# One decoder layer in split fp32: operands moved to one byte offset modulo 256, transposes grouped four to a PSUM bank, and a few tasks listed in another order

## The chip, the cores and the metric

The kernel runs on one core of a Trainium2 chip. The metric is device time in microseconds (us), the median of three runs. Lower is better.

## The reference

One layer of a hybrid decoder on 512 tokens with 1024 features:

```
h = swiglu(rms_norm(x), w_gate, w_up, w_down)      # ffn1, 2816 wide
x = x + 0.5 * rms_norm(h)
u = rms_norm(x)
... = split(u @ w_in)                               # inputs of three token mixers
merged = g0 * (o_nsa @ w_nsa) + g1 * (o_dn @ w_dn) + g2 * (o_mem @ w_mem),  g = sigmoid(u @ w_branch_gate)
x = x + rms_norm(merged @ w_out)
h = swiglu(rms_norm(x), ...)                        # ffn2
x = x + 0.5 * rms_norm(h)
```

The three mixers are an 8-head sparse attention over compressed, selected and window keys, a gated DeltaNet with 4 heads of 128, and a 4-head cross-attention into 256 memory tokens. Everything is fp32 outside; all weights are read once.

## The kernel before

**Split products.** Every large product is done as three matmuls in the type fp32r. Each operand is split into a rounded part (hi, made by ScalarE) and a rest (lo, made by VectorE or GpSimd), and `mm3` (L114 to L119) issues hi x hi (L117), hi x lo (L118) and lo x hi (L119). A weight tile of 128x512 comes through `wload` (L89 to L110): a DMA into `wraw`, a ScalarE copy into `whi` (L106), a subtraction into `wlo` (L109).

Two patterns use `mm3`. In `prod_fm` the weights are the stationary operand (128 columns of `whi` or `wlo`) and the tokens move (`xth`, `xtl`, `odh`, `omth`, `onh`: 256 or 512 columns). In `down_half` the hidden parts `Hh`, `Hl` are stationary and the weights move (512 columns). So each matmul reads two SBUF operands: its moving one, and, while it streams, the stationary one of the matmul after it is being loaded.

**The fast phase.** From the fifth feature tile on, each FFN forms its gate and up products from seven smaller products instead of eight (`fast_tile`, L419 to L450): per feature tile 7 products x 4 slices x 3 = 84 matmuls of 256 columns, all at L429. Their stationary operands lie in two sets of tiles used in turn (`fset`, and `fxth` with `fxtl`), cut out by `fast_set` at an offset of OFFW elements; the moving ones are `thi` and the low parts in `txa`, `txb`, `tmth`, `tmtl`. 16 tiles in each of the two FFNs go this way.

**Where the operands lie.** SBUF pools are laid out one behind the other in each partition, so a tile's byte offset is the sum of the sizes ahead of it. The pool `cp` holds `xth` and `xtl`, then `RB`, then `mth` (2144 fp32 elements = 8576 bytes = 33.5 x 256), then `mtl`; the pools with weights, hidden tiles and the mixers come behind `mtl`. In the built program the offsets modulo 256 are:

| operand | before |
|---|---|
| `xth`, `xtl`, `mth` (also `odh`, `omth`, `tmth`), `ringh` | 0 |
| `mtl` (also `odl`, `omtl`, `tmtl`), `thi`, `txa`, `txb`, `onh`, `onl` | 128 |
| `whi`, `wlo`, `Hh`, `Hl` | 128 |
| set `fset` | 64 |
| set `fxth`, `fxtl` | 192 |

(`ringh` is the buffer for the moving weights of ffn2's down products, laid over `xtl`.) All strides in these operands are multiples of 512 bytes, so the offset modulo 256 is that of every slice.

**Transposes.** `transp` (L190 to L204) turns normalised tokens into features. For each feature tile k it takes a PSUM bank, transposes two token tiles into half of it (L198), and empties it with ScalarE into hi (L200), VectorE into lo (L201) and in some places ScalarE once more into a full fp32 copy (L203). It is called in seven places: the start of ffn1 (`feat`, twice four times), the memory tokens, the mixers' input (twice), and the input of ffn2 (twice).

**Order.** Work is issued as tasks in lists (`order_s` at the start, `order0` around ffn1's end, `order` and `order2` in the mixers, `order3` behind them). `off` lifts some of them by a priority offset, and a scheduler lays out each engine's instructions from that. All loads go through SyncE's queue (SP).

Of the kernel before, what the change touches and what calls it, by code (L numbers as in the profile page):

```python
# [10 lines left out]
F32 = mybir.dt.float32  # L11
# [19 lines left out]

C_ID, C_TRI, C_NEG, C_LVL, C_EYE, C_END = 0, 128, 256, 384, 768, 1024
M_BM, M_HB = 0, 8
PAD = 88


PRM = {'order': ['i', 'a', 'w', 'c01', 'h01', 'r0', 'c00', 'c10', 'c02', 'l0', 'h00', 'h02', 'c12', 'k0', 'h10', 'c11', 'c22', 'h12', 'h11', 'h22', 'r1', 'k1', 'l1', 'c21', 'h21', 'b0', 'e0', 'z', 'c20', 'r2', 'h20', 'c32', 'k2', 'l2', 'c31', 'd00', 'h31', 'r3', 'd01', 'l3', 'b1', 'd02', 'x0', 's00', 'e1', 'd10', 'c30', 'h32', 'x1', 'd11', 's01', 'h30', 's02', 's03', 'q3', 'p0', 'd12', 'o0', 'p1', 'q0', 'p2', 'p3', 'k3', 's10', 'p4', 'q1', 'p5', 's11', 'p6', 'p7', 's12', 's13', 'o1', 'q2', 'f'], 'dma': {'l': 'sync', 'b': 'sync', 'd': 'scalar', 'c': 'sync', 'r': 'sync'}, 'off': {'b0': 300, 'h31': 400, 'r1': 50, 'h32': 50, 'h11': 100, 'h12': 200, 'd10': 100, 'A01': 100, 'A10': 100, 'A11': 100, 'A20': 400, 'A31': 100, 'A21': 20, 'x0': 20, 'x1': 20, 'L': 200, 'S310': 400, 'S001': 20, 'S311': 400, 'A30': 100, 'r0': 400, 'd02': 20, 's11': 100, 'V20': 400, 'l3': 100, 'q1': 20, 'f': 400, 'l1': 50, 'h20': 100, 'h22': 100, 'r3': 50, 'P010': 50, 'y': 100, 'h02': 50, 'S101': 20, 'A00': 100, 'Q0': 50, 'Q1': 200, 'Q2': 50, 'Q3': 50, 'P110': 400, 'V31': 400, 'd01': 200, 'o0': 400, 'p0': 50, 'p1': 400, 'p2': 400, 'p4': 400, 'p5': 400, 'p6': 400, 'p7': 400, 'b1': 200, 'h01': 100, 'M15': 20, 'P201': 400, 'e0': 100, 'e1': 100, 'o1': 20, 'q0': 50, 'q2': 20, 'h21': 20, 'd11': 50, 'p3': 400, 'U0': 100, 's13': 50, 'c11': 20, 's00': 200, 'P011': 400, 'M14': 200, 'c20': 50, 'k2': 20, 'M03': 20, 'V00': 400, 'V01': 400, 'V10': 400, 'V11': 400, 'V21': 400, 'V30': 400, 'l2': 200, 'h00': 400, 'G0': 20, 'S210': 20, 'P101': 200, 'i': 100, 'G2': 20}, 'ph': 'e', 'po': 'ss', 'xpd': (0, 1, 2), 'order2': ['K1', 'K0', 'B', 'M10', 'Q0', 'C0', 'Q1', 'S000', 'S001', 'P000', 'C3', 'P001', 'C1', 'S010', 'P010', 'C2', 'S011', 'V00', 'Q2', 'S101', 'S100', 'P011', 'S110', 'V01', 'M12', 'P100', 'W0', 'P101', 'S111', 'Q3', 'P110', 'S200', 'S210', 'V10', 'P111', 'V11', 'P200', 'M14', 'M15', 'S201', 'P201', 'S211', 'W1', 'V20', 'P211', 'P210', 'V21', 'S301', 'W2', 'S300', 'S311', 'M11', 'P300', 'P301', 'L', 'M13', 'S310', 'G0', 'V30', 'M16', 'G2', 'P311', 'M17', 'P310', 'V31', 'W3', 'A00', 'M00', 'A01', 'G1', 'U0', 'M05', 'A10', 'A11', 'G3', 'A30', 'A31', 'U3', 'U1', 'M03', 'M06', 'A20', 'A21', 'U2', 'M07', 'M22', 'M20', 'M02', 'M24', 'M27', 'M21', 'M23', 'M01', 'M25', 'M04', 'M26'], 'order0': ['d0', 'p0', 'n0', 't0', 'd1', 'k2', 'k0', 'p2', 'p3', 'v', 'k3', 'n1', 'k1', 't1'], 'order3': ['s2', 's3', 's7', 's6', 's5', 's1', 's0', 's4', 'd00', 'd01', 'd11', 'g', 'p0', 'd10', 'n0', 't0', 'p1', 'n1'], 't3': (('mm', 'r'), ('e', 's')), 'pool': {'W2': 2, 's13': 3, 'k0': 0, 'k1': 0, 'k2': 0, 'k3': 2, 'p3': 1, 'C0': 1, 'C1': 0, 'C2': 0, 'C3': 2, 'S310': 0, 'L': 3, 'd11': 3, 'p0': 1, 'p1': 1, 'p2': 1, 'p4': 2, 'p5': 1, 'p6': 1, 'p7': 1, 'S311': 0, 'h01': 0, 'h00': 2, 'h02': 0, 'h10': 0, 'h11': 0, 'h12': 0, 'h22': 0, 'h21': 0, 'h20': 0, 'h31': 0, 'h30': 3, 'h32': 0, 'i': 2, 'P011': 2, 'c21': 0, 'd01': 2, 'S000': 0, 'S001': 0, 'S010': 0, 'S011': 0, 'S100': 0, 'S101': 0, 'S110': 0, 'S111': 0, 'S200': 0, 'S201': 0, 'S210': 0, 'S211': 0, 'S300': 0, 'S301': 0, 'M24': 2, 'G2': 2, 'A01': 0, 'M10': 0, 'M15': 2, 'M12': 2, 'M14': 2, 'M13': 2, 'M17': 2, 'M11': 2, 'M16': 2, 'M23': 0, 'M27': 3, 'M01': 2, 'M00': 2, 'M03': 0, 'M07': 2, 'M06': 1, 'M22': 2, 'M04': 2, 'M20': 2, 'M26': 2, 'M02': 0, 'M21': 2, 'M25': 2, 'M05': 2, 'c11': 1, 'o1': 3, 'P000': 2, 'P001': 1, 'P010': 2, 'P100': 2, 'P101': 2, 'P110': 2, 'P111': 2, 'P200': 2, 'P201': 2, 'P210': 2, 'P211': 2, 'P301': 0, 'P300': 3, 'P310': 2, 'P311': 2, 'c12': 3, 'b1': 1, 'x0': 0, 'x1': 0, 'V21': 0, 'c30': 0, 'c01': 0, 'c02': 0, 'c00': 0, 'c10': 0, 'c22': 0, 'c20': 0, 'c31': 0, 'c32': 0, 's01': 3, 'A31': 0, 'd12': 0, 'y': 2, 'G0': 2, 'G1': 2, 'G3': 0, 'U3': 0, 'W3': 2, 'r1': 2, 's12': 3, 'U2': 0, 'Q0': 2, 'Q1': 2, 'Q2': 2, 'Q3': 1, 's00': 3, 's02': 2, 's03': 3, 's10': 2, 's11': 3, 'e1': 2, 'd00': 1, 'U0': 0, 'U1': 0, 'l2': 0, 'd02': 2, 'K1': 3, 'V11': 0, 'V00': 2, 'r2': 0, 'l3': 3}, 'pool3': {'d00': 3, 'd01': 3, 'd10': 3, 'd11': 0, 'p1': 2, 't1': 3, 't0': 3, 's5': 2, 's7': 2, 's1': 2, 's0': 2, 's3': 2, 's6': 2, 's2': 2, 's4': 2, 'q0': 1}, 'pool0': {}, 'off0': {'p3': 20, 'n1': 50, 'k2': 400, 'k1': 20, 'p2': 100, 'p0': 400}, 'off3': {'s1': 20, 's5': 200, 'g': 200, 't0': 200, 'd10': 200, 'p0': 200, 'n0': 200}, 'tt': ('e', 's'), 'order_s': ['t00', 'w010', 'w000', 't01', 'P00', 'w110', 'y', 'w100', 'P10', 't02', 'w011', 'w001', 't03', 'P01', 'w111', 'w101', 'R0', 'F000', 'P11', 'x', 'n', 't10', 'F200', 't11', 'F101', 't12', 't13', 'F110', 'B', 'F211', 'F011', 'c'], 't0': ('e', 's'), 'rs': ((0, 0), (0, 0)), 'ra': (1, 1), 'warm': 8, 'pools': {'F000': 0, 'F101': 0, 'F200': 0, 'F011': 0, 'F110': 0, 'F211': 0, 'w10': 0, 'w11': 1, 't00': 0, 't01': 0, 't02': 0, 't03': 0, 't13': 0, 't10': 0, 't11': 0, 't12': 0, 'w00': 0, 'w01': 0, 'w000': 0, 'P01': 0}, 'ptc': 'vvs', 'cva': 'v', 'offs': {'t13': 100, 'R1': 400, 't03': 20, 't02': 20, 'w001': 100}, 'vnc': 's', 'sp3': 0, 'hsc': 'vv', 'sf2': 2, 'psc': 'vvvv', 'sp1': 0, 'vbs': 'v', 't1c': 'vs', 'sgv': 256}


class Body:  # L40
    def __init__(self, ctx, tc, a, out, tap):
        self.tc, self.nc, self.a, self.out, self.tap = tc, tc.nc, a, out, tap
        pool = lambda name, **k: ctx.enter_context(tc.tile_pool(name=name, **k))
# [146 lines left out]
    def transp(self, xs, which, hi, lo, tbs, tags=("e",), ks=range(KT), full=None):  # L190
# [4 lines left out]
        for k in ks:  # L195
            pt = self.bank(tags[k % len(tags)], "ptr")
            for i, b in enumerate(tbs):
                nc.tensor.transpose(pt[:, i * P : (i + 1) * P], xs[b][:, k * P : (k + 1) * P], self.ident)  # L198
# [1335 lines left out]
```

## Time and profile before

| | us |
|---|---|
| median of 3 runs (1342.34 to 1346.00) | 1344.37 |
| the profiled execution | 1346.39 |
| its span, first to last instruction | 1344.6 |
| TensorE (PE) busy | 1316.8 (98%) |
| VectorE (DVE) busy | 904.3 (67%) |
| ScalarE (ACT) busy | 713.2 (53%) |
| GpSimd (POOL) busy | 139.5 (10%) |
| mean busy share of the DMA engines | 42% |

1.8 us of the profiled execution lie outside its span. Matmuls are pipelined: a row gives each about 0.17 us more than the step to the next one, so the rate is read from the distance between starts, not from the durations. TensorE's granted clock is 0.999 of 2.4 GHz over the span.

### The profile page before, as it was taken

The numbers are of one execution on the slowest core, as the hardware profiler recorded it, in microseconds if no ns is written. First come the engines' busy times: TensorE is split into PE (matmuls) and PEld (weight loads), VectorE is DVE, ScalarE is ACT, GpSimd is POOL, SyncE is SP. The second block draws the span as 40 slices with busy tenths as digits, with TensorE's granted clock in tenths as the row PEclk, the third lists the DMA queues.
The fourth block names the chain that finished last, engine by engine and source line by source line (L and its number), as shares of the span: only waits on it lengthen the run. The fifth ranks groups of instructions, "written<-read, shape, count | busy, mean of one in ns | idle before, by whom it ended". The sixth has DMA issues, their size and how long they took to land.

```text
span 1344.6 us, 21791 instructions
## 1 busy us (share of the span) xinstructions
PE 1316.8 (98%) x7839; PEld 1124.6 (84%) x7839; DVE 904.3 (67%) x1805; ACT 713.2 (53%) x1536; POOL 139.5 (10%) x126
## 2 busy tenths in 40 slices
PE   8999999999999899999999999999999999999997
PEld 7889999788887778787777877888788899998886
DVE  6897876778567866846887333322788778766765
ACT  7566664767456444316655334333585556646642
POOL 0020000000012222003110212333200000000000
PEclk9999999999999999999999999999999999999999
DMA  7643331577664341323121222533735433317673
GB/s 242 208 150 115 103 119 33 179 253 244 190 189 119 92 123 49 105 87 120 54 70 33 79 71 71 188 95 110 250 119 164 129 107 111 110 33 255 208 223 105
DMA packets 106301, 178.32 MB, mean 133 GB/s; under 512 B 18781, under 2 KB 28369, under 8 KB 106193
## 3 DMA queue, kind: packets, MB, share of 16 engines
q1 hardware_dynamic: 105904, 176.67, 41.9%
q8 instruction: 61, 1.00, 0.3%
q14 instruction: 48, 0.39, 0.1%
q10 hardware_dynamic: 288, 0.26, 0.1%
HBM read 166.84 MB, written 10.01 MB: 132 GB/s over the span
## 4 chain that ended last, share of the span: by engine, by line
PE 85%; DVE 6%; DMA 4%; ACT 2%; issue 2%; SPq 1%; POOL 0%; DVEq 0%; ACTq 0%
PE smm L429 10%; PE pfm L117 7%; PE pfm L118 7%; PE pfm L119 7%; PE se L429 7%; PE ss L429 3%; PE acc_s L119 2%; PE acc_s L117 2%; PE acc_s L118 2%; PE ps L1039 2%; PE sr L429 2%; PE so L429 1%; PE acc_e L118 1%; DVE wlo L109 1%; PE acc_e L119 1%
## 5 line engine op out<-in xcount | busy, mean ns | idle before, releaser
L106 ACT CAST whi<-wraw 128x512 fp32r<-128x512 f32 (+1 forms) x314 | 190.8, 615 | 177.7 <-PE pfm L119 65.1
L109 DVE TENSOR_TENSOR wlo<-wraw,whi 128x512 fp32r<-128x512 f32 (+1 forms) x271 | 188.7, 704 | 108.4 <-ACT whi L106 103.4
L117 PE MATMUL pfm<-xth,whi 128*128 128x512 f32 x384 | 156.1, 409 | 1.5 <-ACT whi L106 1.0
L118 PE MATMUL pfm<-xth,wlo 128*128 128x512 f32 x384 | 154.4, 404 | 0.6 <-DVE wlo L109 0.6
L119 PE MATMUL pfm<-xtl,whi 128*128 128x512 f32 x384 | 154.5, 404 | 0.0
L117 PEld LDWEIGHTS pfm<-xth,whi 128*128 128x128 f32 x384 | 72.3, 189 | 19.2 <-issue 2.8
L118 PEld LDWEIGHTS pfm<-xth,wlo 128*128 128x128 f32 x384 | 72.4, 189 | 15.6 <-DVE wlo L109 1.1
L119 PEld LDWEIGHTS pfm<-xtl,whi 128*128 128x128 f32 x384 | 72.4, 188 | 14.8 <-issue 0.2
L106 ACT CAST ringh<-ringr 128x512 fp32r<-128x512 f32 x82 | 50.0, 620 | 44.1 <-DMA ringr<-in_ffn_d_dram 11.0
L109 POOL TENSOR_TENSOR wlo<-wraw,whi 128x512 fp32r<-128x512 f32 (+1 forms) x40 | 49.9, 1247 | 191.2 <-ACT whi L106 178.4
L429 PE MATMUL smm<-thi,fset 128*128 128x256 f32 x384 | 69.4, 279 | 0.0
L109 DVE TENSOR_TENSOR wlo<-ringr,ringh 128x512 fp32r<-128x512 f32 x75 | 51.2, 690 | 18.7 <-PE acc_e L119 8.2
L429 PEld LDWEIGHTS smm<-thi,fset 128*128 128x128 f32 x384 | 58.5, 188 | 0.2
L445 DVE TENSOR_TENSOR up<-smm,s 128x256 f32<-128x256 f32 x32 | 13.6, 424 | 66.5 <-ACT se L442 66.5
L429 PE MATMUL smm<-thi,fxtl 128*128 128x256 f32 x192 | 53.5, 279 | 0.6 <-DVE fxtl L411 0.6
L429 PE MATMUL smm<-thi,fxth 128*128 128x256 f32 x192 | 53.3, 277 | 0.0
L429 PE MATMUL se<-thi,fset 128*128 128x256 f32 x256 | 46.7, 280 | 0.0
L1042 ACT ACTIVATE Pm<-Pm,nm 128x128 f32<-128x128 f32 (+1 forms) x64 | 35.6, 558 | 14.2 <-DVE nm L1041 13.8
L123 DVE TENSOR_TENSOR Hl<-H,Hh 128x256 fp32r<-128x256 f32 x88 | 35.0, 421 | 6.9 <-ACT Hh L122 5.7
L402 DVE TENSOR_TENSOR fs<-fq 128x1024 f32<-128x1024 f32 x32 | 39.0, 1220 | 0.8 <-DMA fq<-in_ffn_u_dram 0.8
L429 PEld LDWEIGHTS se<-thi,fset 128*128 128x128 f32 x256 | 39.1, 187 | 0.0
L429 PEld LDWEIGHTS smm<-thi,fxtl 128*128 128x128 f32 x192 | 36.1, 188 | 1.0 <-DVE fxtl L411 1.0
(565 smaller groups left out, 3918.0 us busy)
## 6 DMA issues: line engine op xcount, KB each, us to landing
wraw<-in_ffn_d_dram SPq DMA_DIRECT2D x94, 256.0 KB, 2.9
ringr<-in_ffn_d_dram SPq DMA_DIRECT2D x82, 256.0 KB, 3.0
fq<-in_ffn_g_dram SPq DMA_DIRECT2D x64, 256.0 KB, 2.8
fq<-in_ffn_u_dram SPq DMA_DIRECT2D x64, 256.0 KB, 3.1
wraw<-in_w_gate_dram SPq DMA_DIRECT2D x48, 256.0 KB, 2.7
wraw<-in_ffn_u_dram SPq DMA_DIRECT2D x34, 256.0 KB, 3.2
wraw<-in_ffn_g_dram SPq DMA_DIRECT2D x34, 256.0 KB, 3.3
woraw<-in_w_out_dram SPq DMA_DIRECT2D x32, 256.0 KB, 3.9
```

Source lines behind the costliest of these rows:

```text
L106: nc.scalar.copy(hi, raw)
L109: eng.tensor_tensor(lo, raw, hi.bitcast(F32), op=OP.subtract)
L117: t.matmul(out, lh, rh, start=first, stop=False)
L118: t.matmul(out, ll, rh, start=False, stop=False)
L119: t.matmul(out, lh, rl, start=False, stop=last)
L123: return self.nc.vector.tensor_tensor(lo, src, hi.bitcast(F32), op=OP.subtract)
L402: add = lambda *x: v.tensor_tensor(*x, op=OP.add)
L429: m = lambda x, y, **kw: te.matmul(out, x, y, skip_group_check=True, **kw)
L445: v.tensor_tensor(up[:, 256:], a, s7, op=OP.add)
L1039: te.matmul(s[:, : max(n, 256)], A[:, qb * P : qb * P + P], K[j][:, : max(n, 256)], start=j == 0, stop=j == 1)
L1042: nc.scalar.activation(pm, pm, AF.Exp, bias=nm[:, qb : qb + 1], scale=-1.0, accum_out=sm[:, qb : qb + 1])
```

## The change

- OFFW goes from 48 to 16 elements, and the tile `mth` grows by 32 elements to 34 x 256 bytes (the table `rw` in it keeps its size). So everything behind `mth` moves by 128 bytes. Offsets modulo 256 in the built program:

| operand | before | after |
|---|---|---|
| `xth`, `xtl`, `mth`, `odh`, `omth`, `tmth`, `ringh` | 0 | 0 |
| `mtl`, `odl`, `omtl`, `tmtl`, `thi`, `txa`, `txb`, `onh`, `onl` | 128 | 0 |
| `whi`, `wlo`, `Hh`, `Hl` | 128 | 0 |
| set `fset` | 64 | 64 |
| set `fxth`, `fxtl` | 192 | 64 |

- `transp` takes one bank for two feature tiles: four transposes fill it, then ScalarE and VectorE empty its two halves.
- In the task lists: `w` (two small loads) goes ahead of `i` and `a`; `k2` comes behind `d00`; `n1` goes ahead of `v`; `w000` comes first; `t03` and `t02` go ahead of `P10`; `t12` goes ahead of `F200`. The entry `'h01': 1` of the table `pool` lets GpSimd do `wload`'s subtraction in that task, in which there is no `wload`.

```
-PRM = {'order': ['i', 'a', 'w', 'c01', ... 'k2', 'l2', 'c31', 'd00', 'h31', ...
+PRM = {'order': ['w', 'i', 'a', 'c01', ... 'l2', 'c31', 'd00', 'k2', 'h31', ...
...
-        for k in ks:
-            pt = self.bank(tags[k % len(tags)], "ptr")
-            for i, b in enumerate(tbs):
-                nc.tensor.transpose(pt[:, i * P : (i + 1) * P], xs[b][:, k * P : (k + 1) * P], self.ident)
-            g = self.gpre[:, which, k : k + 1]
-            i1 = nc.scalar.activation(hi[:, k, t], pt[:, : n * P], AF.Copy, scale=g)
-            i2 = nc.vector.scalar_tensor_tensor(lo[:, k, t], pt[:, : n * P], g, hi[:, k, t].bitcast(F32), op0=OP.mult, op1=OP.subtract)
-            if full:
-                nc.scalar.activation(full(k), pt[:, : n * P], AF.Copy, scale=g)
+        for k0 in ks[::2]:
+            pts = self.bank(tags[k0 // 2 % len(tags)], "ptr").rearrange("p (j t) -> p j t", j=2)
+            for j in range(2):
+                for i, b in enumerate(tbs):
+                    nc.tensor.transpose(pts[:, j, i * P : (i + 1) * P], xs[b][:, (k0 + j) * P : (k0 + j + 1) * P], self.ident)
+            for j in range(2):
+                k, pt = k0 + j, pts[:, j]
+                g = self.gpre[:, which, k : k + 1]
+                i1 = nc.scalar.activation(hi[:, k, t], pt, AF.Copy, scale=g)
+                i2 = nc.vector.scalar_tensor_tensor(lo[:, k, t], pt, g, hi[:, k, t].bitcast(F32), op0=OP.mult, op1=OP.subtract)
+                if full:
+                    nc.scalar.activation(full(k), pt, AF.Copy, scale=g)
...
-    OFFW = 48
+    OFFW = 16
...
-        rw = oh[:33, 4 * 504 :].rearrange("p (h r) -> p h r", h=NH)
+        rw = oh[:33, 4 * 504 : 4 * 504 + P].rearrange("p (h r) -> p h r", h=NH)
...
-("mth", 4 * 504 + P), ("mtl", 4 * 504)
+("mth", 4 * 504 + P + 32), ("mtl", 4 * 504)
```

ScalarE's first instructions, before: `xth<-ptr` empties a bank of transposes (hi), `whi<-wraw` makes the hi part of a weight tile that the first matmuls wait for.

```order
L200 ACTIVATE xth<-ptr,gpre 128x256 x3
L106 CAST whi<-wraw 128x512 x2
L200 ACTIVATE xth<-ptr,gpre 128x256
L106 CAST whi<-wraw 128x512 x3
L200 ACTIVATE xth<-ptr,gpre 128x256
```

After:

```order
L203 ACTIVATE xth<-ptr,gpre 128x256 x2
L106 CAST whi<-wraw 128x512
L203 ACTIVATE xth<-ptr,gpre 128x256
L106 CAST whi<-wraw 128x512
L203 ACTIVATE xth<-ptr,gpre 128x256
L106 CAST whi<-wraw 128x512 x3
```

The first weight tile's copy moves ahead of the third bank half, and the second one, for which the first matmul waits, stands behind three halves and one copy. In the built program a half can be read only when all four transposes of its bank are done, and ScalarE's read of the second half waits for VectorE's read of the first.

TensorE where the memory tokens (`xm`) are transposed, between the matmuls of ffn1's first down product (`acc_mm`), before:

```order
L198 MATMUL ptr<-cst,xm 128x128 x4
...
L198 MATMUL ptr<-cst,xm 128x128 x2
L119 MATMUL acc_mm<-wlo,Hh 128x512
L198 MATMUL ptr<-cst,xm 128x128 x2
L117 MATMUL acc_mm<-whi,Hh 128x512
L118 MATMUL acc_mm<-whi,Hl_2804 128x512
L119 MATMUL acc_mm<-wlo,Hh 128x512
```

After:

```order
L199 MATMUL ptr<-cst,xm 128x128 x8
L118 MATMUL acc_mm<-whi,Hl_2805 128x512
L119 MATMUL acc_mm<-wlo,Hh 128x512
...
L119 MATMUL acc_mm<-wlo,Hh 128x512
L199 MATMUL ptr<-cst,xm 128x128 x8
L117 MATMUL acc_mm<-whi,Hh 128x512
```

The sixteen transposes stood in groups of four and two; now they stand in two groups of eight, with eleven matmuls of `acc_mm` between them.

## Rows read from the trace of the kernel before

**Rows 1.** The page: its first line, the busy time of each engine, and the chain of work that ended last by engine.

```profile
span 1344.6 us, 21791 instructions
PE 1316.8 (98%) x7839; PEld 1124.6 (84%) x7839; DVE 904.3 (67%) x1805; ACT 713.2 (53%) x1536; POOL 139.5 (10%) x126
...
PE 85%; DVE 6%; DMA 4%; ACT 2%; issue 2%; SPq 1%; POOL 0%; DVEq 0%; ACTq 0%
```

**Rows 2.** Busy time by stretch: the fast phase of ffn1, and the stretch of the DeltaNet with the start of the attention. Columns: the stretch and its length; busy us and number of instructions of PE, PEld, DVE, ACT, POOL; granted clock; DMA share; GB/s.

```profile
62.00:242.00 180.00, 179.62 (x1443) 174.16 (x1441) 139.37 (x165) 104.12 (x208) 7.01 (x2) 1.00 0.33 104
372.00:600.00 228.00, 219.36 (x1306) 181.47 (x1304) 158.92 (x417) 100.33 (x237) 38.02 (x42) 1.00 0.38 110
```

**Rows 3.** What TensorE waited for, longest first: total us, times, longest. The first row and the longest for a weight tile.

```profile
PE ptk L678 <- DVE qs L671: 2.7, 2, 1.6
...
PE pfm L117 <- ACT whi L106: 1.0, 1, 1.0
```

**Rows 4.** The chain of work in order of time, over two feature tiles of the fast phase: start us, length us, what. Each row is one product of 12 matmuls; the first seven use the set `fset`, the next seven the set `fxth`/`fxtl`; the last row is the start of the tile behind them.

```profile
164.25 1.36 PE smm L429 x12
165.61 1.40 PE so L429 x12
167.02 1.41 PE smm L429 x12
168.43 1.42 PE se L429 x12
169.85 1.41 PE smm L429 x12
171.26 1.41 PE ss L429 x12
172.67 1.41 PE se L429 x12
174.09 1.36 PE smm L429 x12
175.45 1.40 PE sr L429 x12
176.85 1.41 PE smm L429 x12
178.26 1.37 PE se L429 x12
179.63 1.36 PE smm L429 x12
180.99 1.36 PE ss L429 x12
182.35 1.36 PE se L429 x12
183.71 1.13 PE smm L429 x10
```

**Rows 5.** TensorE's timeline, start us first, pairs of rows of 512-column matmuls with only matmuls of the same kind left out between them: 30 steps of ffn1's down product, 14 steps of a mixer's input product, 3 and then 8 steps of a merge product, 30 steps of ffn2's down product.

```profile
352.04 0.39 PE L119 MATMUL acc_s<-wlo,Hh 128*128 128x512 f32 x1
...
358.84 0.39 PE L119 MATMUL acc_s<-wlo,Hh 128*128 128x512 f32 x1
...
417.40 0.39 PE L118 MATMUL pfm<-xth,wlo 128*128 128x512 f32 x1
...
420.65 0.39 PE L117 MATMUL pfm<-xth,whi 128*128 128x512 f32 x1
...
801.85 0.39 PE L117 MATMUL pfm<-onh,whi 128*128 128x512 f32 x1
...
802.55 0.39 PE L117 MATMUL pfm<-onh,whi 128*128 128x512 f32 x1
...
804.36 0.39 PE L119 MATMUL pfm<-onl,whi 128*128 128x512 f32 x1
...
1299.97 0.39 PE L117 MATMUL acc_e<-ringh,Hh 128*128 128x512 f32 x1
...
1306.84 0.39 PE L117 MATMUL acc_s<-ringh,Hh 128*128 128x512 f32 x1
```

**Rows 6.** Groups of TensorE's matmuls by shape: count | busy us, mean ns of one | idle before.

```profile
L118 PE MATMUL pfm<-xth,wlo 128*128 128x512 f32 x384 | 154.4, 404 | 0.6 <-DVE wlo L109 0.6
L118 PE MATMUL acc_e<-ringh,Hl 128*128 128x512 f32 x44 | 17.3, 393 | 0.0
```

**Rows 7.** The timeline of the program's start: ScalarE's first copy of a weight tile, TensorE's first two matmuls, and two rows with 24 steps of 256-column matmuls between them.

```profile
7.04 0.61 ACT L106 CAST whi<-wraw 128x512 fp32r<-128x512 f32 x1
...
7.70 0.38 PE L117 MATMUL pu<-xth,whi 128*128 128x256 f32 x1 [0.64 <-ACT whi L106]
...
8.71 0.39 PE L117 MATMUL pg<-xth,whi 128*128 128x256 f32 x1 [0.62 <-ACT whi L106]
...
9.04 0.28 PE L119 MATMUL pu<-xtl,whi 128*128 128x256 f32 x1
...
11.90 0.28 PE L117 MATMUL pu<-xth,whi 128*128 128x256 f32 x1
```

**Rows 8.** The instructions that empty the banks of the transposes: count, duration ns least/median/most, first and last start us.

```profile
L200 ACT ACTIVATE xth<-ptr,gpre x48: 452/475/536, 5.8 to 1005.1; 128x256 fp32r<-128x256 f32 x48
L201 DVE SCALAR_TENSOR_TENSOR xtl<-ptr,gpre,xth x48: 473/479/486, 6.3 to 1005.7; 128x256 fp32r<-128x256 f32 x48
```

More of the change, by code (lines that the diff above doesn't have):

```diff
@@ L1177, in run @@
             with tc.tile_pool(name="wx0", bufs=1) as self.wx:
-                dt, dc, load, part = self.bias_table([self.cp.tile([P, n], F32, tag=t, name="room") for t, n in (("mth", 4 * 504 + P), ("mtl", 4 * 504))])
+                dt, dc, load, part = self.bias_table([self.cp.tile([P, n], F32, tag=t, name="room") for t, n in (("mth", 4 * 504 + P + 32), ("mtl", 4 * 504))])
                 step, full = self.fast_tokens(xh, xl, RB, H[:, FT - 16 :])
```

2 lines of the change are left out of this document (1 added, 1 removed).

## The prediction

> **What bounds the kernel now.** I read the page first: TensorE is busy 98% of the span, and the chain that ended last runs through TensorE for 85% of it [rows 1]. Then the waits: the longest that TensorE has on any pair of lines is 2.7 us, and on weight tiles, the main supply, 1.0 us [rows 3]. So the kernel is a stream of matmuls, and its time is the number of matmuls times the step from one start to the next. In the fast phase of ffn1 that holds without a gap: 179.62 of 180 us, VectorE at 139.37 and ScalarE at 104.12 [rows 2]. In the mixers it holds less: 219.36 of 228 us, and the chain there hops between engines [rows 2].
>
> The step itself is what this change touches. Rows 4 show the same work, products of 12 matmuls of 256 columns with equal shapes, at two rates: 1.36 us (113.3 ns a step) and 1.41 us (117.5 ns). Which one it is follows the operands. With the set `fset` (offset 64, moving operand at 128) a tile keeps the 1.36 of the tile before it for one product, and from the second on stays at 1.40 to 1.42; with the other set (192 against 128) five of seven products run at 1.36 or 1.37, and only the two that move `tmth`, which lies at 0, take 1.40 and 1.41 [rows 4]. So a product is fast when weights minus moving operand is 64 modulo 256 throughout, slow at 192, and slow when its two moving parts lie at different offsets. After a mixed product the other set finds back to 1.36, and `fset` doesn't.
>
> The 512-column matmuls show the same [rows 5]. ffn1's down product has both operands at 128 (difference 0): 6.80 us for 30 steps, 226.7 ns. A mixer's input product has 0 and 128 (difference 128): 3.25 us for 14 steps, 232.1 ns. A merge product holds the proof within one loop: right after matmuls with difference 128, its first 3 steps take 0.70 us (233 ns); its operands `onh` and `onl` have difference 0, and the next 8 steps take 1.81 us (226 ns). In ffn2's down product two of each three steps have difference 128: 6.87 us for 30, 229.0 ns on average.
>
> The change makes every difference of split products 0, or 64 in the fast phase.
>
> **The change part by part.**
>
> *Fast phase.* Two tiles take 183.71 - 164.25 = 19.46 us. All 14 products at 1.36 make 19.04, so 0.42 us less for a pair, and 16 pairs in the two FFNs give -6.7 us. If all ran at 1.41 instead, a pair would take 19.74, and the sum is +4.5. I take the first: 64 was the fast difference, and no mixed offsets are left to break the rhythm. Nothing hides this: TensorE never waits there.
>
> *512 columns, difference 128 to 0.* Products of `xth` with weights: 3 x 384 in the mixers' group [rows 6], and by the code 336 in 512-wide FFN tiles and 96 for `w_z`, together 1,584. Along the built order about one in seven is followed by a transpose, an fp32 matmul or a wait, which leaves 1,360 steps. Each can lose 232.1 - 226.7 = 5.4 ns at most; the merge product needed 3 of 24 steps to fall into the faster rhythm, so I take 21/24 of it, 4.7 ns: -6.4 us (bounds 0 and -7.3). ffn2's down product: 82 loads in the ring x 2 token tiles x 3 = 492 steps, from 229.0 to 226.7: -1.1. The products of `odh` and `omth`, some 120 steps like the ring's: -0.4. Together -7.9.
>
> *256 columns, difference 128 to 0.* The halves of the first FFN tiles, 480 matmuls, now at 2.86 us for 24 steps, 119.2 ns [rows 7]. No long run of 256 columns at difference 0 stands in the trace. Bounds: no gain, or down to 113.3 as in rows 4, which is -2.8. The 512-column pair is the same loop, but part of these steps lie in the starved beginning, so I take 2 ns: -1.0.
>
> *What the mixers swallow.* About 870 of the 1,360 steps lie between 372 and 850 us, worth 4.1 us. There the chain passes through other engines, which don't get faster. I give half back: +2.0 (bounds 0 and +4.1).
>
> *Transposes.* The same 112 transposes and the same copies remain, of 475 ns on ScalarE and 479 on VectorE for each feature tile [rows 8]. A bank holds two tiles, so it is free 2 x (475 + 479) = 1.9 us after its transposes if nothing overlaps, against 0.95; but two banks are in turn, so four feature tiles still leave at one per 0.48 us. TensorE stands idle only if it reaches its next group earlier. For the memory tokens eleven matmuls of about 227 ns, 2.5 us, lie between the groups; the eight halves of the two engines need 4 x 0.48 plus one lag, 2.4 us. Cover and need are level, so 0 (bounds -1 and +2). At the start the first half waits for four transposes and not two. The first two matmuls begin at 7.70 and 8.71 us, right behind ScalarE's copies [rows 7], and a flowing stream begins with the second. That copy still stands behind three halves and one copy, all of them later by two transposes of some 0.2 us each: +0.5 (bounds 0 and +1).
>
> *The lists.* `w` moves two small loads on SP's queue, some tens of loads ahead of their use; `n1`, `k2`, `t03` and `t12` trade places with neighbours on VectorE and ScalarE. All the waits that they could end or make are of the size of rows 3, one or two us. I take 0 (bounds -1.5 and +1.5). `h01` changes nothing.
>
> *Sum.* -6.7 - 7.9 - 1.0 + 2.0 + 0.5 = -13.1 us on the profiled execution: 1346.4 - 13.1 = 1333.3. That execution lies 2.0 above the median of the three runs, so I forecast a median of **1331.3 us**.
>
> **The rivals.**
>
> *Only half of it is there.* Either the fast phase locks at neither rate cleanly, or the 512-column steps lie at 230 in the midst of a mixer's traffic as in the ring [rows 5]. Either way some 6 or 7 us remain: **1337.5**.
>
> *The addresses do nothing.* Then the two rates come from something that goes along with the sets, and the time is 1346.4 + 0.5 - 2.0 = **1344.9**. Against it: one loop changes its rate within three steps when only its operands change [rows 5], and both sets of rows 4 run the same code. The Trainium skill ("TensorE: Matmul & The Clock Gate", Step-by-step: what each phase is for) says that TensorE has two independent SBUF read ports, so that loading the next weights takes nothing from the running matmul; by that rule offsets couldn't matter, and this rival would hold. The trace disagrees with it by 113.3 against 117.5 ns.
>
> *It is not the difference but the place (the slower side).* Every moving operand with long fast runs lies at 128; the slow ones lie at 0 (`xth`, `ringh`, `tmth`), and the weights of the slow set at 64. After the change all moving operands lie at 0 and the fast phase's weights at 64, a pair that the trace shows only in mixed products, 1.41 [rows 4]. If the place decides, the fast phase goes to 1.41 (+4.5), and the roughly 1,050 steps of down products that run at 226.7 go to 232.1 (+5.7): 1344.9 + 10.2 = **1355**. It decides as soon as those steps lose more than 5 ns each. Against it: `fset` against `thi` at 128 is slow too, so a rule by place needs one exception more than the rule by difference.
>
> *The banks stall.* If TensorE waits at each of 28 fuller banks for 0.5 us, the 13 us are eaten: about **1344**. The built order speaks against it, with 11 to 15 matmuls between groups.
>
> *More than the sum.* The 256-column halves reach 113 and the mixers give nothing back: **1326**.
>
> **How the numbers follow.** Chances: forecast 0.60 (its own range 1327 to 1335), half 0.15, more 0.07, addresses do nothing 0.08, banks stall 0.03, place 0.07. The first three hold 0.82 and reach from 1325 to 1341, which is the range. A measurement of this kernel tells about 0.3%, 4 us, from no change. Faster: the first three, 0.82. Same: nothing and stall, 0.11. Slower: place, 0.07.
>
> **What would show it.** In the fast phase each product of 12 should stand at 1.36 in the chain for both sets, and a pair of tiles at 19.04. `pfm<-xth` should fall from 404 to about 399 ns mean, and ffn2's down product to 226.7 a step. ffn1's down product should stay where it is; if it rises, place decides. The first two matmuls should start about half a microsecond later. New waits of TensorE on `xth`, `mth` or `xtl` would show the banks. I am wrong if the steps fall and the span doesn't: then the mixers' other engines, or the loads in the down products, took the place of TensorE.

## The result

The changed kernel takes 1335.21 us in the median of 7 executions (1333.23 to 1340.92), the kernel before 1346.00 beside it: a ratio of 0.9933, with a 95% interval of 0.9916 to 0.9951. It is faster by 0.7%. The forecast was 1331.3, with a range of 1325 to 1341.

The profiled execution of after is the slowest of its seven, 1340.92 us, span 1339.1. Its page, to be held against [rows 1]:

```profile
span 1339.1 us, 21789 instructions
PE 1310.1 (98%) x7839; PEld 1127.4 (84%) x7839; DVE 902.9 (67%) x1805; ACT 713.6 (53%) x1536; POOL 138.8 (10%) x126
PE 65%; DVE 6%; ACT 2%; DMA 2%; issue 1%; POOL 0%; DVEq 0%; ACTq 0%; SPq 0%
```

TensorE is still the bound, and 6.7 us less busy. (The chain in this trace reaches back only to 319 us and its shares add up to 76%, so its 65% is not to be compared with the 85% of [rows 1].) Where the time went shows when the span is cut at the first and last matmul of each fast phase (L429 before, L432 after; starts from the timeline). The first column is the kernel before; the others are the profiled executions of after and of the kernels of the experiments below.

| us | before | after | e2 | e3 | e4 | e10 | e11 |
|---|---|---|---|---|---|---|---|
| up to the first fast matmul | 69.04 | 72.21 | 69.10 | 72.64 | 70.07 | 68.98 | 71.51 |
| fast phase of ffn1, 1,316 steps | 152.46 | 154.56 | 154.56 | 149.19 | 155.00 | 155.00 | 154.56 |
| from there to ffn2's fast phase | 816.58 | 811.45 | 810.62 | 811.40 | 809.03 | 810.99 | 809.34 |
| fast phase of ffn2, 1,316 steps | 152.46 | 149.19 | 155.00 | 149.19 | 154.99 | 154.56 | 149.20 |
| behind it | 130.02 | 128.03 | 128.04 | 128.05 | 128.03 | 128.07 | 128.06 |
| span without the two phases | 1039.66 | 1035.38 | 1031.44 | 1035.78 | 1030.82 | 1031.72 | 1032.60 |

(The last row also holds 27 steps at the head of each phase, mixed with other work, 24.0 us before and 23.7 in the others.) Two things stand out. The start is 3.2 us later than before. And the two fast phases, with the same code and offsets, ran at two rates: 149.19 / 1,316 = 113.4 ns a step in ffn2, 117.4 in ffn1, where before had 115.9 in both. In what follows the two rates, some 113 and 118 ns, are called the two rhythms.

The chain of work shows ffn2's phase as forecast, every product of 12 at 1.36 us and two tiles at 1098.50 - 1079.46 = 19.04, against 19.46 in [rows 4]:

```profile
1079.46 1.36 PE so L432 x12
1080.82 1.36 PE smm L432 x12
...
1098.50 1.36 PE so L432 x12
```

TensorE's timeline in ffn1's phase shows the rate change in the middle of a stream:

```profile
101.39 0.28 PE L432 MATMUL smm<-thi,fxth 128*128 128x256 f32 x1
...
104.11 0.30 PE L432 MATMUL smm<-thi,fxth 128*128 128x256 f32 x1
104.24 0.28 PE L432 MATMUL smm<-thi,fxtl 128*128 128x256 f32 x1
104.36 0.28 PE L432 MATMUL smm<-txb,fxth 128*128 128x256 f32 x1
...
107.19 0.28 PE L432 MATMUL se<-txb,fxth 128*128 128x256 f32 x1
```

From 101.39 to 104.11 are 24 steps of 113.3 ns. One step then takes 0.13 us; by the program's order this product waits for ScalarE's copy of the same bank. From 104.36 to 107.19 are 24 steps of 117.9 ns, and so it stays for the other 142 us. The granted clock is 1.00 on both sides of the change (the stretches 92 to 104 and 105 to 240 us, columns as in [rows 2]), so the rate is not the clock's:

```profile
92.00:104.00 12.00, 12.00 (x106) 12.00 (x106) 12.00 (x14) 8.65 (x18) 0.00 (x0) 1.00 0.51 153
105.00:240.00 135.00, 135.00 (x1148) 135.00 (x1148) 100.38 (x118) 76.88 (x156) 0.00 (x0) 1.00 0.29 91
```

The 512-column steps, to be held against [rows 5]: a mixer's input product (14 steps), ffn1's down product (30 steps) and ffn2's (30 steps), then the group of [rows 6].

```profile
413.61 0.39 PE L117 MATMUL pfm<-xth,whi 128*128 128x512 f32 x1
...
416.79 0.39 PE L119 MATMUL pfm<-xtl,whi 128*128 128x512 f32 x1
```

```profile
351.61 0.39 PE L119 MATMUL acc_s<-wlo,Hh 128*128 128x512 f32 x1
...
358.41 0.39 PE L119 MATMUL acc_s<-wlo,Hh 128*128 128x512 f32 x1
...
1293.77 0.39 PE L118 MATMUL acc_e<-ringh,Hl 128*128 128x512 f32 x1
...
1300.57 0.39 PE L118 MATMUL acc_e<-ringh,Hl 128*128 128x512 f32 x1
```

```profile
L118 PE MATMUL pfm<-xth,wlo 128*128 128x512 f32 x384 | 153.4, 401 | 0.0
```

3.18 / 14 = 227 ns (232.1 before), 226.7 in ffn1's down product as before, 226.7 in ffn2's (229.0 before). These came as forecast; the mean of `pfm<-xth` fell from 404 to 401 ns, not to 399.

The start, by the waits, the timeline of ScalarE and TensorE, and the stretches (columns as in [rows 2]):

```profile
PE pu L117 <- ACT whi L106: 3.3, 1, 3.3
```

```profile
6.48 0.61 ACT L106 CAST whi<-wraw 128x512 fp32r<-128x512 f32 x1
...
8.66 0.62 ACT L106 CAST whi<-wraw 128x512 fp32r<-128x512 f32 x1 [1.19 <-DMA wraw<-in_ffn_u_dram]
...
9.33 0.58 PE L117 MATMUL pu<-xth,whi 128*128 128x256 f32 x1 [3.26 <-ACT whi L106]
9.71 0.41 PE L117 MATMUL pg<-xth,whi 128*128 128x256 f32 x1
9.92 0.41 PE L118 MATMUL pg<-xth,wlo 128*128 128x256 f32 x1
```

```profile
10.00:15.00 5.00, 5.00 (x25) 5.00 (x25) 1.69 (x4) 1.30 (x3) 0.00 (x0) 0.50 0.81 280
10.00:20.00 10.00, 10.00 (x65) 10.00 (x65) 5.07 (x11) 5.85 (x13) 0.28 (x1) 0.72 0.77 257
```

TensorE's order still has `pu` first, but with `w000` ahead of `w010` in the list `order_s` the load for `pg` now goes out first, and `pu` waits for the second one. TensorE is idle for 3.26 us; behind that its steps take 213 ns, which is the 1.2 GHz level, until 15 us (granted clock 0.50 over 10 to 15 us, where before had 1.00).

### The profile page after: what moved, and what is told of

Same layout as the page of the kernel before. It is cut to its first block, busy times and chain, and to the rows that moved or that the text cites. A ratio compares the mean times of both kernels' runs of the same rounds, so it can differ in the third digit from the quotient of the medians.

```text
span 1339.1 us, 21789 instructions
## 1 busy us (share of the span) xinstructions
PE 1310.1 (98%) x7839; PEld 1127.4 (84%) x7839; DVE 902.9 (67%) x1805; ACT 713.6 (53%) x1536; POOL 138.8 (10%) x126
## 4 chain that ended last, share of the span: by engine, by line
PE 65%; DVE 6%; ACT 2%; DMA 2%; issue 1%; POOL 0%; DVEq 0%; ACTq 0%; SPq 0%
PE pfm L117 7%; PE pfm L119 7%; PE pfm L118 7%; PE smm L432 5%; PE se L432 3%; PE acc_s L119 2%; PE acc_s L117 2%; PE acc_s L118 2%; PE ps L1042 2%; PE ss L432 2%; PE acc_e L119 2%; PE acc_e L118 2%; PE acc_e L117 1%; PE ppt L1064 1%; PE po L1078 1%; DVE wlo L109 1%
## 5 line engine op out<-in xcount | busy, mean ns | idle before, releaser
L117 PEld LDWEIGHTS pfm<-xth,whi 128*128 128x128 f32 x384 | 72.2, 188 | 18.5 <-issue 3.1
L119 PEld LDWEIGHTS pfm<-xtl,whi 128*128 128x128 f32 x384 | 72.2, 188 | 13.5 <-issue 0.2
L432 PE MATMUL smm<-thi,fset 128*128 128x256 f32 x384 | 69.0, 278 | 0.0
L432 PEld LDWEIGHTS smm<-thi,fset 128*128 128x128 f32 x384 | 58.4, 188 | 0.2
L432 PE MATMUL smm<-thi,fxtl 128*128 128x256 f32 x192 | 53.7, 279 | 0.6 <-DVE fxtl L414 0.6
L432 PE MATMUL smm<-thi,fxth 128*128 128x256 f32 x192 | 53.5, 279 | 0.0
L432 PE MATMUL se<-thi,fset 128*128 128x256 f32 x256 | 45.8, 278 | 0.0
L432 PEld LDWEIGHTS se<-thi,fset 128*128 128x128 f32 x256 | 38.8, 188 | 0.0
L432 PEld LDWEIGHTS smm<-thi,fxtl 128*128 128x128 f32 x192 | 36.0, 188 | 1.0 <-DVE fxtl L414 1.0
```

What stands on the lines that cost most here:

```text
L117: t.matmul(out, lh, rh, start=first, stop=False)
L119: t.matmul(out, lh, rl, start=False, stop=last)
L432: m = lambda x, y, **kw: te.matmul(out, x, y, skip_group_check=True, **kw)
```

## The experiments

All times of whole kernels are medians. The kernel before, run beside each of them, had medians of 1343.8 to 1344.9. Only one execution of each kernel is profiled; what its other executions did is inferred from their times.

**e1: the rates by themselves.**

> This kernel leaves the whole layer out. It runs only streams of fp32r matmuls of 256 or 512 columns, two stationary and two moving tiles in turn as in the fast phase, and the difference (stationary minus moving, modulo 256) is set for each stream: 0, 32, ... 224 for both widths, for 256 columns also 16, 48, 80, 112 and, with the moving operand in two other places, 0, 64 and 192. Each stream is three runs of 48 matmuls; between the first two stands one matmul whose moving operand is 128 bytes off, between the last two one of 128 columns. Theory of two rhythms: at a difference of 64 a stream of 256 columns can hold 113 ns a step and 118, and one of the two disturbances changes it from one to the other. Rival, the difference alone sets the rate: at 64 every run stands at 113, at 0 near 119, at 192 near 118, whatever comes between. Rival, the place matters: the rate at the same difference changes with the place of the moving operand. For 512 columns the forecast is 226.7 at 0 and 232 at 128; whether 32, 64 or 96 are below 226.7 is open, and would be worth 6 ns a step if they go down to 220.

Rows of the timeline, each a stretch of one run with its start, its length and its number of matmuls (the trace leaves the numbers out of the names; `c256m0d` has the moving operand at one place, `c256m64d` 64 bytes further). The step is the length, less the own time of the last matmul (0.28 us at 256 columns, 0.39 at 512), over the count less one. The three runs at difference 64, then two of the same difference 64 bytes further, then one at difference 0:

```profile
50.12 4.92 PE L34 MATMUL c256m0d<-mov,wts 128*128 128x256 f32 x42
55.57 5.11 PE L34 MATMUL c256m0d<-mov,wts 128*128 128x256 f32 x42
61.34 5.23 PE L34 MATMUL c256m0d<-mov,wts 128*128 128x256 f32 x43
...
176.62 5.23 PE L34 MATMUL c256m64d<-mov,wts 128*128 128x256 f32 x43
182.39 4.94 PE L34 MATMUL c256m64d<-mov,wts 128*128 128x256 f32 x42
...
27.01 5.19 PE L34 MATMUL c256m0d<-mov,wts 128*128 128x256 f32 x42
```

At 64 the first place gives 113.2, 117.8, 117.9: one matmul with another offset, and the stream is slow from then on. The second place gives 117.9, then 113.7 (its first steps are still slow): a matmul of 128 columns, and it is fast. That matmul came six times at 117.8, at 64 and 192 in three places, and led to 113.3 in two of them. At 192 the streams showed the same two rates (113.3 and 117.8, at the first place only 117.8), at 0 always 119.8 to 119.9, in all three places; 16, 32, 80, 96, 112, 128 and 160 lay between 117 and 120, and 48 and 224 between 116.7 and 118, but for one run of 48 at 123. So the two rhythms are there, in one stream of the same operands, and the place of the operands changes no rate. For 512 columns, at differences 0, 64, 128 and 192:

```profile
256.73 9.46 PE L34 MATMUL c512m0d<-mov,wts 128*128 128x512 f32 x41
323.71 9.96 PE L34 MATMUL c512m0d<-mov,wts 128*128 128x512 f32 x42
391.69 10.16 PE L34 MATMUL c512m0d<-mov,wts 128*128 128x512 f32 x43
459.02 10.24 PE L34 MATMUL c512m0d<-mov,wts 128*128 128x512 f32 x44
```

226.8, 233.4, 232.6 and 229.1 ns, unmoved by the disturbances. 0 is the best there, and the open hope for 220 is gone.

**e2: the offsets alone.** OFFW 16 and the longer `mth` in the kernel before, nothing else.

> The kernel before with the offsets alone: OFFW 16 and the longer mth, with the old transposes and the old lists. By the prediction's sum the offsets bring 6.7 + 7.9 + 1.0 - 2.0 = 13.6 us of gain, so 1331 in the median. By the trace after, which shows the whole change at 1335 with a start 3.2 us later, the offsets bring 12 to 14 and the start takes 3 of it: 1332, with the first matmul of weights at 7.7 us and the granted clock at 1.00 from there. If the offsets are worth only what the whole change brought, this run stands at 1335. The theory of two rhythms adds: the fast phases of the two FFNs stand at 113 or 118 ns a step each, and the times of single executions spread over 6 us or more (1,344 steps of 4.5 ns in one phase); the rival, that something in ffn1 alone makes its phase slow, expects 118 in ffn1 and 113 in ffn2 again in this run.

1332.36 us (1331.40 to 1342.79), ratio 0.9921 [0.9897, 0.9945]. By the table its span without the fast phases is 1031.44, 8.2 less than before, with the fast phase of ffn1 beginning where it did. Of the expected start the first matmul came (7.24 us), the clock did not: behind waits of 1.2 and 0.45 us, 15 steps took 213 ns (granted clock 0.84 over 10 to 15 us). Its profiled execution had both phases near 118 and took 1342.79; the other five lie at 1331.4 to 1333.4, 10 us below. Two phases of 155 against two of 149.2 are 11.6. The theory of something slow in ffn1 falls: here ffn2 was slow too, from the wait at its head on (TensorE waits there for VectorE's `fxtl`, in the third product of the first fast tile), and ffn1 from the place where after's fell.

**e3: the old list at the start, the banks of after.** The whole list `order_s` is that of before; the cut shows its head.

```diff
-'order_s': ['w000', 't00', 'w010', 't01', ...
+'order_s': ['t00', 'w010', 'w000', 't01', ...
```

> The kernel after with the list order_s of before, so that the first load of weights is again the one for the first product (pu), and the transposes stay in the new banks. If the exchange of the first two loads is what makes the start late, the first matmul of weights begins at 8.2 us or earlier and not at 9.3, the granted clock in 10 to 20 us is 1.00 and not 0.72, and the median is 2.5 to 3.5 us under that of the whole change: about 1332. If the fuller banks make it late, the first matmul stays at 9 us or later and the median at 1335. As to the fast phases: two rhythms expect either rate in either phase; something in ffn1 expects 118 there again.

1335.69 us. The first matmul came at 6.85 us, but the fast phase began at 72.64, and the time is that of after. The loss had moved, as the waits show:

```profile
PE pg L117 <- DVE sg L303: 3.0, 1, 3.0
```

At about 22 us TensorE waits for VectorE's `sg`, and from 25.5 to 28.7 us its steps take 213 ns, the 1.2 GHz level. So the exchanged loads are not the whole cause. Both phases were at 113 in the profile: ffn1's is not slow by itself.

**e4: the old banks, the lists of after.**

> The kernel after with the old transposes (one feature tile per bank), all else as after. The offsets alone gave 1332.4, the whole change 1335.2, the whole change with the old list at the start 1335.7. If the fuller banks cost the 3 us, this run stands at 1332 to 1332.5, its first matmul of the fast phase near 69 us (before 69.0, after 72.2) and the granted clock in the first 30 us near 1.00. If the new list order_s costs them by itself (it exchanges the first two loads, and the first product waits for the second), this run stays at 1335 and its fast phase begins near 72.

1343.07 us (1333.57 to 1346.60), at first sight a refutation: 11 us above e2. The table says why it is none: without the phases this execution takes 1030.82, the least in the table, and both phases stand at 155.0. Why most executions of this kernel are slow is not shown. TensorE's wait for `pu` is still there, 2.47 us instead of 3.26, again with steps of 213 ns behind it, and the fast phase begins at 70.07, between the two forecasts. By the four starts, one execution each (69.1 old and old, 70.1 lists, 72.6 banks, 72.2 both), the fuller banks cost 2 to 3.5 us at the start and the exchanged loads 1 or nothing. The start with old lists and banks varied by 1.6 us between kernels that differ only behind it (67.7 in e7, 69.2 in e12), so these are rough.

**e5 and e6: the difference in the kernel.** The offsets alone with OFFW 48 (difference 192) and with OFFW 0.

> The offsets alone, with OFFW back at 48: both sets at 192, the moving operands at 0, so the difference is 192 throughout the fast phase. By the prediction's rule 192 is the slow difference: 117.5 to 118 ns a step in both phases, 2,640 steps x 4.4 ns = 11.6 us over the clean 1332, so 1344 in every execution. By the streams, which held 113.3 and 117.8 at 192 as at 64, the two are alike: single executions lie between 1332 and 1344, in steps of about 5.8 us for each phase that falls to 118.

> The offsets alone, with OFFW 0: all operands at 0, so the difference is 0 in the fast phase too. The streams showed 119.8 ns at 0, in all three places and whatever came between: 2,640 steps x 6.5 ns = 17.2 us over the clean 1332, so 1349, with no scatter between executions (within 2 us of each other). If the difference did not matter in the kernel (other traffic sets the rate), it would stay at 1332 to 1343.

e5: 1343.86 us; ten of eleven executions lie at 1342.7 to 1346.7, one at 1340.3. e6: 1349.01, from 1346.8 to 1350.2. The chain of work, e5 and then e6, in ffn2's phase:

```profile
1085.46 1.41 PE smm L429 x12
1086.87 1.41 PE sr L429 x12
```

```profile
1084.10 1.44 PE smm L429 x12
1085.54 1.44 PE ss L429 x12
```

At 0 both phases took 157.9 us, 120.0 ns a step, and the median is the forecast one (1349); the executions spread over 3.4 us where 2 were expected. At 192 the kernel nearly always takes the slow rhythm, by the times of its executions and both phases of the profiled one (155.0), though the streams could hold the fast one.

**e7: one short wait taken away.** In e2, ScalarE's copy of `smm` ahead of a cast.

```diff
-        nc.scalar.copy(u, a)
+        self.copied = nc.scalar.copy(u, a)
...
-                nc.scalar.copy(hi[:, c.start + j], x[:, j])
+                q1 = nc.scalar.copy(hi[:, c.start + j], x[:, j])
+                if f == 9 and not i:
+                    self.order(q1, self.copied)
```

> The offsets alone, with ScalarE's copy of smm (L438) in the second fast tile put ahead of one cast of the next weights, for which TensorE was late there by 10 to 20 ns. If this small wait is what throws the stream from 113 to 118, the step there (124 to 133 ns in the traces so far) is 113, the phase of ffn1 keeps the rate it has ahead of that place in the profiled execution, and at most the start of a phase can still choose the slow rhythm; median 1332, and fewer executions above 1336 than one in six. Rival: the rhythm falls at random places, and the profiled execution shows a change from 113 to 118 somewhere else.

1338.43 us (1329.83 to 1343.33), and six of eight executions above 1336: the expectation fails. In the profiled execution both phases were at 117.8 from the wait at their head on. There is no long step in it, but nor is there in the phases of the other kernels that begin at 117.8 (ffn2 in e2, ffn1 in e10), so it does not show whether the edit removed it. The late product can throw the stream (e10 below), but the wait at the head of a phase decides as well.

**e8: what moves the rhythm.**

> This kernel leaves the whole layer out. It runs one stream of 256-column matmuls at a difference of 64, with the moving operand at 0 as in the kernel's fast phase, in runs of 24. Between the runs stands one disturbance, four times in a row for each kind: a matmul of fewer columns (16 to 240), a matmul split in two, a matmul whose moving operand lies 32 to 224 further, twelve matmuls of which each third lies 128 further (as the mixed products of the kernel before), and, 36 times, a wait for a copy by VectorE of 64 to 240 columns. Theory of two rhythms: each run of 24 stands at 113.3 or at 117.8 ns a step from its second or third step to its end, a disturbance can move it either way, and runs behind waits of different lengths come out both ways, which is how a wait of some ns more or less at the start of a phase can decide 5.8 us. Rival: behind a wait the stream always takes one and the same rhythm, and then the phases that began at 117.8 must have another cause. Open, and of use: whether one kind of disturbance leads to 113.3 from either rhythm.

Of the 35 runs that a wait really preceded, 29 stood at 113.3 and 6 at 117.8. Three neighbours, two behind copies of 192 columns and one behind a copy of 208:

```profile
524.73 2.99 PE L35 MATMUL waitx<-mov,wts 128*128 128x256 f32 x24 [0.45 <-DVE junk L67]
528.17 3.09 PE L35 MATMUL waitx<-mov,wts 128*128 128x256 f32 x24 [0.45 <-DVE junk L67]
531.73 2.99 PE L35 MATMUL waitx<-mov,wts 128*128 128x256 f32 x24 [0.47 <-DVE junk L67]
```

24 matmuls take 3.09 us behind one wait, 2.99 behind another of the same 0.45 us and behind one of 0.47. So either rhythm can follow a wait, and the length of the wait does not decide it by itself. Of the disturbances, a matmul of 128 columns led here from either rhythm to the other (four of four, where e1 had two of six), splits and most moved operands left 113.3 alone, and so did the twelve mixed matmuls (four of four); one of 112 columns led once from 117.8 to 113.3 and then kept it three times.

**e9: a try to set the rhythm**, with e2 and the whole change run again beside it.

```diff
         prod(q7, self.S_S3, self.T_T3, True)
+        if f < 10:
+            te.matmul(banks[1][:, 256:368], hi[:, 0, :P], T[0][0][:, 0, :112], start=True, stop=True, skip_group_check=True)
```

> The offsets alone, with one matmul of 112 columns more behind the second product of the first four feature tiles of each fast phase (it writes 112 columns of a bank that nobody reads). In the streams such a matmul led from 117.8 to 113.3 and left 113.3 as it was, at a cost of 51 ns: 8 x 0.05 = 0.4 us in all. Theory of two rhythms: both phases stand at 113.3 from the fourth tile on in every execution, whatever the waits ahead of it do, so the executions lie within 3 us of each other at 1332 (span without the two phases 1031.4, phases 149.6 each, 1.8 around). Rival, the rhythm is lost again at random, or the one passage from 117.8 to 113.3 in the streams was luck: executions scatter from 1331 to 1343 as those of the offsets alone.

> The offsets alone once more, on the chip and in the call of the runs beside it. Its executions should fall into groups, near 1332 with both phases at 113, near 1337 with one at 118, near 1343 with both at 118, as those of the two looks at nearly this kernel did, whose medians were 1332.4 and 1338.4. If the groups are not there and all lie near one time, the scatter between those looks had another cause than the rhythm.

> The whole change once more, on the chip and in the call of the runs beside it. Span without the two fast phases 1035.4, which is 4 us more than with the offsets alone, so its groups should lie near 1335.5 with both phases at 113 and 1341 with one at 118, and its first matmul of the fast phase near 72.2 us, against 69 or less. If the fuller banks cost nothing, its best execution equals that of the offsets alone.

e9: 1332.26 us, ratio 0.9909 [0.9894, 0.9924], the lowest median of all kernels. But its profiled execution (1337.07) had ffn1's phase at 113.3 and ffn2's at 117.8 right through its four short matmuls: the one passage in e8 did not come again, as the rival said, and the executions spread over 7 us. Its lead over e2 is not a measured one (1332.26 against 1332.36 and, in e10, 1333.36).

e10: 1333.36 us; its six executions are 1331.25, 1331.80, 1332.32, 1334.39, 1336.42 and 1343.07. e11: 1337.16, from 1331.87 to 1340.20 without a gap. The groups show roughly for the offsets alone, with 1334.39 between two of them, and not for after. The mark set for e11, that its best execution equals that of the offsets alone if the fuller banks cost nothing, is met within 0.6 us (1331.87 against 1331.25), though its fast phase begins 2.5 us later and its span without the phases is 0.9 us longer. The chain of e10's profiled execution holds the fall in ffn2's phase, at the product that waits for ScalarE's copy:

```profile
1068.01 1.36 PE smm L429 x12
1069.37 1.36 PE se L429 x12
1070.73 1.43 PE smm L429 x12
1072.15 1.41 PE ss L429 x12
```

The same place of the program, the fifth product of the second fast tile, is where the ffn1 phases of after, e2 and e11 fell, while e3 in both phases, after's ffn2 and e11's ffn2 passed it with a step of 131 to 133 ns and came back to 113. The steps at the four falls were 124, 129, 133 and 133 ns, so the length of the step does not decide it. The profiled executions at a difference of 64 (after, e2, e3, e4, e7, e9, e10, e11) hold 16 phases: 7 stand at 117.8 from the wait at their head on, 9 at 113.3; of these 4 fall at that one place, and none changes its rhythm anywhere else, but for the steps right at e9's short matmuls.

**e12: mixed offsets back.**

```diff
-... p.tile([P, 2, 4, 256], F32R, tag=t, ...) for p, t in (..., (self.cp, "mth"), ...)
+... p.tile([P, 2048 + m], F32R, tag=t, ...)[:, m:]... for p, t, m in (..., (self.cp, "mth", 32), ...)
```

> The offsets alone, but the low parts tmth lie 128 bytes further, so that two of the seven products of every fast tile, of either set, move operands at two offsets again (difference 64 and 192 in turn), as the products of set fxth did in the kernel before. There the stream came back to 113.3 behind the two mixed products in every tile of that set. If the mixed products pull the stream back, both phases run at some 114.6 ns a step (5 products of 12 at 113.3 to 113.8, two at 117.5): 150.8 us a phase against 149.2 clean and 155.0 slow, and the executions lie within 3 us of each other around 1335 (1031.5 without the phases + 301.6 + 1.8). Rival: nothing pulls back, a phase that begins at 117.8 stays there: 155 a phase, executions from 1334 to 1343 as those of the offsets alone.

1342.62 us, from 1341.6 to 1346.1: little scatter, but at the slow end, 155.0 in both phases. Both theories miss. Mixed products go with the slow rhythm here, in all eleven executions, where in [rows 4] one set came back to 1.36 behind them and in e8 they left 113.3 alone.

## Why the prediction was right, and where it was not

The median lies inside the range, 3.9 us above the forecast. The offsets are the cause, as forecast: alone they give the whole gain (e2), and the 512-column part of the sum was right in mechanism and size. The fast phase was right in size only for executions in which both phases are fast. The sum took that for certain, because no mixed offsets are left to break the rhythm; the wait at the head and one late product break it as well, so how near the median came is in part luck. Against the profiled execution (-13.1 forecast, -5.5 found):

- *Fast phase, -6.7.* A phase that holds 113.4 is worth 3.27 us, two make -6.5, and e3 has that. In after's profiled execution ffn1's gave +2.1 and ffn2's -3.3. The step that failed is the reading of [rows 4] that 64 is the fast difference and 192 the slow one; the first product of `fset`, at 192, stood at 1.36 there too. Both differences hold 113.3 and 117.8 (e1), though the kernel at 192 was nearly always slow (e5); at 0 there is one rate, about 120. The bound of +4.5 for two slow phases, which I set aside, was real: +4.6 in e2, +5.1 in e4.
- *512 columns, -7.9.* From all starts in the traces of before and e2, steps times gain: products of `xth` and `xtl` 6.2 (6.4 forecast), ffn2's down product 1.1 (1.1), `odh` and `omth` 0.4 (0.4), and some 0.5 in `onh`, in the products of `mth` and in those of 288 columns, not forecast: 8.2. ffn1's down product gained nothing, as forecast.
- *256-column halves, -1.0.* The step that failed is the gain itself: they went from 119.0 to 119.8 ns, +0.4, and e1 shows 119.8 as the rate at 0. I had moved part of the 512-column gain to a shape whose trace had none.
- *What the mixers swallow, +2.0.* Nothing, so this term was too large by its whole size. Outside the phases e2 is 8.2 us shorter than before, about all that the steps gave.
- *Transposes and start, +0.5; lists, 0.* The step that failed is the one on the start. It let the second weight copy be late by the transposes alone; but the list exchanged the loads, TensorE's order did not follow, and that copy waited 1.19 us for its load. The stream itself began only 0.6 us later than before's (9.33 against 8.71). The larger part came behind the idle stretch: some 25 steps at 213 instead of 119 ns, 2.3 us by estimate, a cost that I had not put in. Together +3.2 in after. How it divides between banks and lists is rough (e4).

With both phases fast, after would take 1035.4 + 2 x 149.2 + 1.8 outside the span = 1335.6 by its first profile, near its median, and 1332.8 by the span of e11; e2 would take 1331.6, within 1 us of its own median. So by these two profiles the fuller banks and the lists together cost after 1 to 4 us, where the spans without the phases of the kernels with the old banks and lists differ by 1.7 among themselves (1030.1 in e7 to 1031.8 in e5, without before and e12, whose offsets are mixed). That a slow phase in about half of its executions makes up the rest is an estimate from their times.

Of the rivals, "half only" was nearest in mechanism: it said that the fast phase might lock at neither rate cleanly. "The addresses do nothing" is out: OFFW alone moves the median from 1332 to 1349. The rule of the Trainium skill ("TensorE: Matmul & The Clock Gate", Step-by-step: what each phase is for) that loading the next weights takes nothing from the running matmul does not fit e1: 226.8 against 233.4 ns, by the offset alone. That the two reads get in each other's way is one reading of it, not shown. The pair that the prediction held against the rule, 113.3 and 117.5, is no evidence, since one difference has both rates. "Place" is out: the down product that went from 128 to 0 stayed at 226.7, and e1's rates are the same in three places. "The banks stall" had a part, seen at the start only (from ffn1's fast phase to ffn2's, after is 0.8 us longer than e2). "More than the sum" comes to 1327.5 by its own terms (-1.8 and -2.0), not 1326.

What stays open: what picks the rhythm at the end of a wait and at the late product, why one set of the kernel before came back to 113 in every tile while e12 never did, and how to force it. No kernel here does, and the 10 us between executions of e2 remain.

## What to carry to other kernels

Place moving operands and weights of 512-column fp32r products at the same offset modulo 256, but not those of 256-column ones, whose rate at 0 was among the slowest (119.8 ns). Then measure the phases of a kernel apart, since a stream of identical matmuls can run at two rates and one profile shows only one of them. When a median moves, cut the span at landmarks first: e4 looked like a loss of 11 us and was the shortest in the table outside the two fast phases. When loads are put in another order, look whether the engine that waits for them still takes them in that order.

## What was not expected of the hardware

- A stream of 256-column fp32r matmuls at a difference of 64 or 192 has two stable rates, 113.3 and 117.8 ns. Either can follow a wait of the same 0.45 us (e8); a single step of 124 to 133 ns threw four phases from 113.3 to 117.8, while steps of 131 to 133 ns left others at 113.3; and a rate then held, in after for 142 us.
- The same offset for both operands is best at 512 columns (226.8 ns) and among the slowest at 256 (119.8 ns).
- 512-column streams have one rate for each difference: 226.8 ns at 0, 229.1 at 192, 232.6 at 128, 233.4 at 64.
- An idle stretch of 3.26 us at the start was followed by steps of 213 ns, half the clock, for some 5 us; in e2 15 such steps came behind waits of 1.2 and 0.45 us, before had no such stretch behind two waits of 0.6.
